# Second down phase built like the first: left factors from the stored hidden tiles, weight differences put aside earlier

## The chip, the cores and the metric

The kernel runs on one core of one Trainium2 chip. The metric is the time of one execution on the device in microseconds (us). Five engines with queues of their own take part: PE (TensorE, matmuls; PEld is its weight load), DVE (VectorE), ACT (ScalarE), POOL (GpSimd; here mainly the queue for stores) and SP (SyncE; the queue for loads). Transfers of all queues run on 16 DMA engines.

## The reference, cut to what matters

One residual block over 1024 tokens of width 1024; all float32:

```python
x = x + 0.5 * swiglu(rmsnorm(x, ffn1_norm), ffn1_w_gate, ffn1_w_up, ffn1_w_down)
x = x + hybrid_mixer(rmsnorm(x, mix_norm), ...)
x = x + 0.5 * swiglu(rmsnorm(x, ffn2_norm), ffn2_w_gate, ffn2_w_up, ffn2_w_down)
out = rmsnorm(x, final_norm)

def swiglu(h, w_gate, w_up, w_down):
    return (silu(h @ w_gate) * (h @ w_up)) @ w_down      # 1024 -> 2816 -> 1024
```

The change touches the last `swiglu` alone: how its hidden values (2816 x 1024 tokens) and `ffn2_w_down` (2816 x 1024) reach the last product.

## The kernel before, in words

**Precision.** A float32 operand is split into a rounded high part (a CAST on ACT, L169) and the rest (a subtraction on DVE, L170); a product is three matmuls (high by high, high by low, low by high), recorded at L91.

**Seven products.** Large matrix products are done in 2x2 blocks with seven products instead of eight (Strassen-Winograd). The factors are named P1, P2, P3, P5, P6, P7 and Q4. Three of the seven (P1, P2, P3) take blocks as they are on the right side, the other four take sums or differences. `Blocks.product` accumulates them in four PSUM banks, and small DVE and ACT steps combine the banks.

**Gate-up phase.** The 2816 hidden features are 22 tiles of 128. Three are made by plain products, two by a joint unit, and 17 one after another by a `Unit` of 84 matmuls of 128x512 (7 products x 4 k-tiles x 3). Gate and up weights come through `L` (`Loads`), two buffers named `raw`: a `raw` is loaded again when its last reader is done. `left` splits the weights and forms their sums (L482, L484, L485). Each unit leaves a hidden tile in two halves of 512 tokens. `Aside.take` gets them: two neighbouring tiles (a pair, 11 pairs in all) are combined by four subtractions or additions on DVE (L647), and the seven results are stored to the DRAM tensor `c_sp` from POOL (`put`, L644).

**Down phase.** `down` runs 16 turns. A turn is one group of 128 output rows and its partner four groups on, over two or three pairs: seven products in the order P1 P7 P5 P6 P2 Q4 P3, with 6 or 9 matmuls each (42 or 63 a turn, 924 in all). While a turn runs, `Prep` makes the left factors of the next turn and some right factors; the right factors of the first two pairs are made in the last unit of gate-up. Turns that are not the last of their group add their results to DRAM by accumulating stores from POOL (L835). Turns 12 to 15 are the last of their groups: they combine the banks with the loaded sums on DVE (L875) and hand the rows on (`ready`).

**The two down phases differ.** In the first (`i` = 0), the output rows are features: the left factors come from `ffn1_w_down`, four blocks loaded two turns ahead into `raw` and combined on DVE (L482, L484, L485); the right factors are the hidden differences read back from `c_sp[0]`, 512 columns at a time (`rights_back`, four tiles ahead). In the second (`i` = 1), the output rows are tokens. Its left factors are the hidden differences, read from `c_sp[1]` in pieces of 128 columns (`left_back`, L509: 7 x 2 or 3 pieces a turn, loaded within the turn ahead into the `w` tiles that the splits use). Its right factors come from `ffn2_w_down`, one 1 MB load for each pair into `raw`, with four DVE subtractions there (`rights_rows`, L771).

After each of the last turns, `to_output` squares, scales and stores rows of the final result (L1382 to L1402).

**What sets the order.** The program names its steps in the order of the functions below. The framework then fixes each engine's order when the program is built, by that order and by its own estimates of when operands and buffers will be there, so that an instruction may stand ahead of its place. On the chip each engine takes its instructions in that fixed order. `s` is a pool of 72 tiles of 128x512, `w` one of 10 tiles of 128x1024.

Of the kernel before, what the change touches and what calls it, by code (L numbers as in the profile page):

```python
# [41 lines left out]
def hybrid_block(ctx: ExitStack, tc: tile.TileContext, t: dict):  # L42
# [136 lines left out]
    class Loads:  # L179
# [14 lines left out]
        def take(self):  # L194
            return self.raw.pop(0)
# [176 lines left out]


# [10 lines left out]
    def ffn_weights(i, pre, nstd):  # L384
        wg, wu, wd = (t[f"{pre}_w_{n}"][0] for n in ("gate", "up", "down"))
        for m in range(int(i == 0), nstd):
            for w in (wg, wu):
                yield [part(0, w[:, m * P : (m + 1) * P])]
        for m in range(nstd, NF):
            yield [part(j * S, w[:, m * P : (m + 1) * P]) for j, w in enumerate((wg, wu))]  # L390
        for j, (g, q0, q1) in enumerate(TURNS):
            if i:
                continue
            n = (q1 - q0) * P
            rows = wd[2 * q0 * P : 2 * q1 * P].rearrange("(k two p) c -> two p k c", two=2, p=P)
            yield [(b * n, n, (lambda a: a.rearrange("p (k c) -> p k c", c=P)),
                    rows[two, :, :, d * P : (d + 1) * P])
                   for b, (two, d) in enumerate(((1, g), (0, g), (1, g + 4), (0, g + 4)))]
        for q in range(NQ * i):
            yield [part(0, wd[2 * q * P : 2 * (q + 1) * P])]  # L400

# [101 lines left out]
    def left_back(g, q0, q1):  # L503

        a = {}
        n = (q1 - q0) * P

        def load(to, i):
            nc.sync.dma_start(out=to.rearrange("p (k c) -> p k c", c=P),  # L509
                              in_=c_sp[1][i, q0:q1, :, g * P : (g + 1) * P].rearrange("k p c -> p k c"))  # L510

        def begin(i):
            raw = w4(F32)[:, : 2 * n]
            for j in range(2):
                load(raw[:, j * n : (j + 1) * n], i + j)
            return raw

        yield a
        raw = begin(0)
        yield  # L520
        for i, after_it in ((0, 4), (4, 2), (2, 6)):
            now = raw
            if after_it < 6:
                raw = begin(after_it)
            else:
                raw = s()[:, :n]
                load(raw, 6)
            parts = split(w4()[:, : 2 * n], w4()[:, : 2 * n], now)
            for j in range(2):
                a[FACTORS[i + j]] = tuple(x[:, j * n : (j + 1) * n] for x in parts)  # L530
            yield
        a["Q4"] = split(s(F32R)[:, :n], s(F32R)[:, :n], raw)
        yield

# [97 lines left out]

    class Aside:

        def __init__(self, i):
            self.sp, self.op = c_sp[i], ALU.add if i else ALU.subtract
            self.names = (("P1", "P5", "P2", "P3", "P7", "P6", "Q4"), ("P1", "P7", "P2", "Q4", "P5", "P6", "P3"))[i]
            self.raw = 0, 2, 3, (1 if i else None)  # L640
            self.even = {}

        def put(self, j, i, x):
            nc.gpsimd.dma_start(out=self.sp[FACTORS.index(self.names[i]), j], in_=x)  # L644
# [4 lines left out]

        def take(self, m, hf, x):  # L650
            j, odd = divmod(m, 2)
            if not odd:
# [3 lines left out]
                else:  # L656
                    self.e1 = x
                    self.t1 = self.comb(s(), self.e0, x, self.op)
# [4 lines left out]
            else:  # L663
# [3 lines left out]
                t3 = self.comb(self.e1, x, self.e1, self.op)  # L667
                self.put(j, 4, t3)
                t4 = self.comb(s(), t2, self.o0, self.op)
# [5 lines left out]
    def gate_up(i, act, started, nstd):  # L675
# [50 lines left out]
        for m in range(nstd + 2, NF):  # L726
# [4 lines left out]
            else:  # L731
                prep = iter(())
                makers[i] = Prep(i)
                makers[i].begin(0)
            for n, name in enumerate(FEW):
                unit.do(name)
                next(prep, None)
                if i in makers:
# [9 lines left out]
    def rights_back(ahead=4):  # L748
# [4 lines left out]
        def load():  # L753
            q, name = todo[len(raws)]
            raws.append(s())
            nc.sync.dma_start(out=raws[-1], in_=c_sp[0][FACTORS.index(name), q])
# [7 lines left out]
    def rights_rows():  # L764


        def done(name, x):
            b[name] = split(s(F32R), s(F32R), x)

        def comb(out, x, y, op):  # L770
            nc.vector.tensor_tensor(out=out, in0=x, in1=y, op=op)  # L771
            return out

        for q in range(NQ):
            b = ring[q] = {}
            raw, _ = L.take()
            b11, b12, b21, b22 = (raw[:, i * HALF : (i + 1) * HALF] for i in range(4))
            done("P1", b11)
            comb(b11, b11, b12, ALU.subtract)
            yield  # L780
            done("P7", comb(b12, b22, b12, ALU.subtract))
            yield
            done("P5", b11)
            yield
            done("P6", comb(b11, b11, b22, ALU.add))
            yield
            done("P2", b21)
            comb(b21, b11, b21, ALU.subtract)
            yield
            done("Q4", b21)  # L790
            yield
            done("P3", b22)
            L.load()
            yield

    class Prep:


        def __init__(self, i):
            self.i, self.made, self.lefts = i, 0, iter(())  # L800
            self.rights = rights_rows() if i else rights_back()
# [6 lines left out]
        def begin(self, j):  # L808
            if j < len(TURNS):
                g, q0, q1 = TURNS[j]  # L810
                self.lefts = left_back(g, q0, q1) if self.i else left(L.take()[0], (q1 - q0) * P, "P3")
# [619 lines left out]
```

## Time and profile before

| what | value |
|---|---|
| median of 3 runs | 1896.9 us (1896.22 to 1897.58) |
| the profiled execution's own time | 1896.36 us |
| its span, first to last instruction | 1894.7 us |
| mean granted TensorE clock | 0.986 |
| PE busy | 1833.0 us, 97% |
| DVE busy | 1381.2 us, 73% |
| ACT, POOL busy | 893.5 us, 252.4 us |

The engine rows overlap in time. What ends the execution is read from where the fullest engine, PE, does not run or runs slowly. The profiled execution lies 0.5 us under the median. The first down phase lies at about 474 to 689 us of the span, the second gate-up at about 1218 to 1641 us, the second down phase at 1641 to 1886 us.

### The profile page before, as it was taken

The numbers are of one execution on the slowest core, as the hardware profiler recorded it, in microseconds if no ns is written. First come the engines' busy times: TensorE is split into PE (matmuls) and PEld (weight loads), VectorE is DVE, ScalarE is ACT, GpSimd is POOL, SyncE is SP. The second block draws the span as 40 slices with busy tenths as digits, with TensorE's granted clock in tenths as the row PEclk, the third lists the DMA queues.
The fourth block names the chain that finished last, engine by engine and source line by source line (L and its number), as shares of the span: only waits on it lengthen the run. The fifth ranks groups of instructions, "written<-read, shape, count | busy, mean of one in ns | idle before, by whom it ended". The sixth has DMA issues, their size and how long they took to land.

```text
span 1894.7 us, 23205 instructions
## 1 busy us (share of the span) xinstructions
PE 1833.0 (97%) x8200; PEld 1508.1 (80%) x8200; DVE 1381.2 (73%) x2167; ACT 893.5 (47%) x1602; POOL 252.4 (13%) x400
## 2 busy tenths in 40 slices
PE   6999999999999999999999999999999999989997
PEld 5777888888888878888888878887888888777775
DVE  4788666666777797768787898658766666755768
ACT  3543222223555455667677775524322222344544
POOL 1201101010222221010101000210110101122211
PEclk8999999999999999999999999999999999999998
DMA  7213333334999853241313343412433333598985
GB/s 235 93 56 127 102 106 106 109 97 143 239 232 223 229 195 91 63 100 34 95 45 73 98 136 103 145 47 60 149 107 111 100 98 104 174 196 207 211 192 180
DMA packets 252933, 246.93 MB, mean 130 GB/s; under 512 B 14176, under 2 KB 197008, under 8 KB 252816
## 3 DMA queue, kind: packets, MB, share of 16 engines
q1 hardware_dynamic: 217072, 157.87, 27.8%
q0 software_dynamic: 35744, 87.58, 18.3%
q8 instruction: 64, 1.05, 0.2%
q14 instruction: 53, 0.43, 0.1%
HBM read 150.76 MB, written 85.20 MB: 125 GB/s over the span
## 4 chain that ended last, share of the span: by engine, by line
PE 68%; issue 15%; DVE 7%; DMA 4%; POOL 3%; ACT 1%; SPq 1%; POOLq 0%; DVEq 0%; ACTq 0%
PE ps L91 67%; DMA w<-c_sp 2%; DVE w L170 1%; DVE s L875 1%; POOL r_sp L835 1%; POOL c_sp L644 1%; DVE s L170 1%; DMA s<-c_sp 1%; DVE s L269 1%; PE ps L277 0%; DVE s L176 0%; POOL x_sp L835 0%; ACT w L169 0%; DMA r_sp<-s 0%; DMA raw<-in_ffn_w_gate 0%
## 5 line engine op out<-in xcount | busy, mean ns | idle before, releaser
L91 PE MATMUL ps<-s,w 128*128 128x512 f32 (+1 forms) x6400 | 1527.1, 393 | 38.6 <-ACT s L175 11.8
L91 PEld LDWEIGHTS ps<-s,w 128*128 128x128 f32 x6400 | 1198.2, 189 | 293.7 <-ACT s L175 12.7
L169 ACT CAST w<-raw 128x1024 fp32r<-128x1024 f32 (+2 forms) x158 | 157.5, 998 | 289.1 <-PE ps L91 189.1
L170 DVE TENSOR_TENSOR w<-raw,w 128x1024 fp32r<-128x1024 f32 (+2 forms) x158 | 182.0, 1153 | 109.4 <-PE ps L91 56.0
L91 PE MATMUL ps<-s,s 128*128 128x512 f32 (+3 forms) x944 | 241.4, 382 | 6.0 <-ACT s L858 4.3
L91 PEld LDWEIGHTS ps<-s,s 128*128 128x128 f32 x944 | 177.7, 189 | 46.1 <-ACT s L858 6.5
L644 POOL DMA_DIRECT2D c_sp<-s x154 | 83.5, 542 | 763.1 <-DVE s L630 579.8
L170 DVE TENSOR_TENSOR w<-w,w 128x768 fp32r<-128x768 f32 (+2 forms) x102 | 103.3, 1013 | 78.5 <-ACT w L169 39.3
L170 DVE TENSOR_TENSOR s<-s,s 128x512 fp32r<-128x512 f32 (+2 forms) x181 | 118.6, 670 | 39.8 <-ACT s L169 39.2
L169 ACT CAST w<-w 128x768 fp32r<-128x768 f32 (+2 forms) x102 | 89.6, 878 | 85.1 <-DMA w<-c_sp 39.3
L169 ACT CAST s<-s 128x512 fp32r<-128x512 f32 (+2 forms) x181 | 104.6, 607 | 43.4 <-DMA s<-c_sp 31.6
L626 ACT ACTIVATE s<-s 128x512 f32<-128x512 f32 x38 | 24.1, 633 | 190.0 <-DVE s L625 190.0
L170 DVE TENSOR_TENSOR s<-raw,s 128x512 fp32r<-128x512 f32 (+2 forms) x131 | 86.2, 666 | 25.9 <-ACT s L169 25.5
L482 DVE TENSOR_TENSOR w<-raw 128x1024 f32<-128x1024 f32 (+2 forms) x54 | 60.6, 1124 | 47.7 <-PE ps L91 46.7
L169 ACT CAST s<-raw 128x512 fp32r<-128x512 f32 (+2 forms) x131 | 76.7, 602 | 38.7 <-DVE raw L771 38.6
L611 ACT ACTIVATE s<-ps 128x512 f32<-128x512 f32 x38 | 22.7, 598 | 113.2 <-PE ps L91 113.2
L1254 DVE TENSOR_TENSOR s<-s,ps 128x128 f32<-128x128 f32 (+2 forms) x96 | 52.7, 548 | 16.8 <-ACT s L1250 16.4
L1242 ACT ACTIVATE s<-ps 128x128 f32<-128x128 f32 (+2 forms) x96 | 47.0, 490 | 37.7 <-PE ps L91 37.3
L835 POOL DMA_DIRECT2D r_sp<-s x48 | 41.6, 876 | 149.6 <-ACT s L854 48.3
L1250 ACT ACTIVATE s<-s 128x128 f32<-128x128 f32 (+2 forms) x96 | 50.2, 523 | 20.6 <-DVE s L1246 19.3
L617 DVE TENSOR_TENSOR s<-s,ps 128x512 f32<-128x512 f32 x38 | 26.0, 685 | 45.0 <-PE ps L91 45.0
L835 POOL DMA_DIRECT2D x_sp<-s x48 | 41.6, 866 | 126.3 <-DVE s L860 60.6
(133 smaller groups left out, 1697.6 us busy)
## 6 DMA issues: line engine op xcount, KB each, us to landing
c_sp<-s POOLq DMA_DIRECT2D x154, 256.0 KB, 2.5
raw<-in_ffn_w_gate SPq DMA_DIRECT2D x43, 512.0 KB, 3.9
raw<-in_ffn_w_up SPq DMA_DIRECT2D x43, 512.0 KB, 5.2
x_sp<-s POOLq DMA_DIRECT2D x80, 256.0 KB, 4.5
s<-c_sp SPq DMA_DIRECT2D x77, 256.0 KB, 7.1
r_sp<-s POOLq DMA_DIRECT2D x64, 256.0 KB, 5.1
w<-c_sp SPq DMA_DIRECT2D x72, 192.0 KB, 5.0
raw<-in_ffn_w_down SPq DMA_DIRECT2D x11, 1024.0 KB, 8.9
```

The costliest lines, as they stand in the source:

```text
L91: nc.tensor.matmul(out, lhs, rhs, **kw)
L169: nc.scalar.copy(hi, x)
L170: nc.vector.tensor_tensor(out=lo, in0=x, in1=f(hi), op=ALU.subtract)
L482: nc.vector.tensor_tensor(out=two(y), in0=two(blk(1, 2)), in1=blk(3).unsqueeze(1).to_broadcast([P, 2, n]), op=ALU.add)
L611: last_silu[0] = nc.scalar.activation(self.s0, o, AF.Silu)
L617: nc.vector.tensor_tensor(out=self.u3, in0=self.u2, in1=self.o[2], op=ALU.add)
L626: last_silu[0] = nc.scalar.activation(self.u2, self.u2, AF.Silu)
L644: nc.gpsimd.dma_start(out=self.sp[FACTORS.index(self.names[i]), j], in_=x)
L835: nc.gpsimd.dma_start(out=self.acc(self.g + 4 * i, hf), in_=x, accum_op=ALU.add)
L1242: behind(nc.scalar.activation(u["s"][:, cols], u["z"][:, cols], AF.Exp), table_set)
L1250: nc.scalar.activation(sc, sc, AF.Ln, bias=1.0)
L1254: nc.vector.tensor_tensor(out=sc, in0=sc, in1=u["z"][:, cols], op=ALU.max)
```

## The change

The second down phase takes the first one's code. `Aside.take` stores each half of a hidden tile as it is, to a new DRAM tensor `l_sp`, in four groups of 128 columns, and does no arithmetic for `i` = 1. `Loads` brings four blocks of `l_sp` for each turn into `raw`, and `left` combines them. The right factors that need a difference of `ffn2_w_down` are made in the gate-up phase: `weights` loads four 128x512 blocks after a unit's first product, `differences` makes four combinations on DVE after its sixth and stores them to `c_sp[1]`. This is done in 11 of the 17 single units. `rights_back` reads those back and takes P1, P2 and P3 from `ffn2_w_down` itself. `left_back` and `rights_rows` are gone.

```diff
+    l_sp = dr.tile([4, 4, P, NQ, P], F32, name="l_sp")
...
         for j, (g, q0, q1) in enumerate(TURNS):
+            n = (q1 - q0) * P
             if i:
+                yield [(b * n, n, (lambda a: a.rearrange("p (k c) -> p k c", c=P)), l_sp[b, g, :, q0:q1, :])
+                       for b in range(4)]
                 continue
...
-        for q in range(NQ * i):
-            yield [part(0, wd[2 * q * P : 2 * (q + 1) * P])]
...
-    def left_back(g, q0, q1):
...
-            nc.sync.dma_start(out=to.rearrange("p (k c) -> p k c", c=P),
-                              in_=c_sp[1][i, q0:q1, :, g * P : (g + 1) * P].rearrange("k p c -> p k c"))
...
+    wd2 = t["ffn2_w_down"][0]
...
+        def weights(self, j):
+            if not self.part or j >= NQ:
+                return
+            self.w = [s() for _ in range(4)]
+            for i in range(4):
+                nc.sync.dma_start(out=self.w[i], in_=wd2[(2 * j + i // 2) * P : (2 * j + i // 2 + 1) * P, hs(i % 2)])
+
+        def differences(self, j):
+            if not self.part or j >= NQ:
+                return
+            b11, b12, b21, b22 = self.w
+            t1 = self.comb(b11, b11, b12, ALU.subtract)
+            self.put(j, 1, t1)
+            t3 = self.comb(b12, b22, b12, ALU.subtract)
+            self.put(j, 4, t3)
+            t2 = self.comb(b22, t1, b22, ALU.add)
+            self.put(j, 5, t2)
+            t4 = self.comb(b21, t2, b21, ALU.subtract)
+            self.put(j, 6, t4)
+
         def take(self, m, hf, x):
             j, odd = divmod(m, 2)
+            if self.part:
+                nc.gpsimd.dma_start(out=l_sp[2 * hf + 1 - odd, :, :, j, :].rearrange("g p c -> p g c"),
+                                    in_=x.rearrange("p (g c) -> p g c", c=P))
+                return
...
+            pair = (m - nstd - 2) * NQ // (NF - nstd - 4)
+            odd = pair == (m - nstd - 1) * NQ // (NF - nstd - 4)
             for n, name in enumerate(FEW):
                 unit.do(name)
                 next(prep, None)
+                if n == 0 and not odd:
+                    out.weights(pair)
+                if n == 5 and not odd:
+                    out.differences(pair)
...
-            nc.sync.dma_start(out=raws[-1], in_=c_sp[0][FACTORS.index(name), q])
+            src = c_sp[part][FACTORS.index(name), q]
+            if part and name in ("P1", "P2", "P3"):
+                m = 2 * q + int(name != "P1")
+                src = wd2[m * P : (m + 1) * P, hs(int(name == "P3"))]
+            nc.sync.dma_start(out=raws[-1], in_=src)
...
-    def rights_rows():
...
-            self.rights = rights_rows() if i else rights_back()
+            self.rights = rights_back(i)
...
-                self.lefts = left_back(g, q0, q1) if self.i else left(L.take()[0], (q1 - q0) * P, "P3")
+                self.lefts = left(L.take()[0], (q1 - q0) * P, "P3")
```

Three places show how the fixed order moves. The first is PE at the start of the second down phase, in turn 1. Before, its P7 and P5 stand as follows (`ps` is the bank of a product, `w` a left factor, `s` a right factor; P7 goes to ps_14260, P5 to ps_14279):

```order
L91 MATMUL ps_14260<-s_13935,w_14172 128x512
L91 MATMUL ps_14260<-s_13936,w_14172 128x512
L91 MATMUL ps_14279<-s_13960,w_14172 128x512
L91 MATMUL ps_14279<-s_13961,w_14172 128x512
L91 MATMUL ps_14260<-s_13935,w_14173 128x512
L91 MATMUL ps_14260<-s_14050,w_14172 128x512
L91 MATMUL ps_14260<-s_14051,w_14172 128x512
L91 MATMUL ps_14260<-s_14050,w_14173 128x512
L91 MATMUL ps_14279<-s_13960,w_14173 128x512
L91 MATMUL ps_14279<-s_14054,w_14172 128x512
L91 MATMUL ps_14279<-s_14055,w_14172 128x512
L91 MATMUL ps_14279<-s_14054,w_14173 128x512
```

In the changed kernel the same two products of turn 1 (P7 in ps_14360, P5 in ps_14376):

```order
L91 MATMUL ps_14360<-s_14025,w_14262 128x512
L91 MATMUL ps_14360<-s_14026,w_14262 128x512
L91 MATMUL ps_14360<-s_14025,w_14263 128x512
L91 MATMUL ps_14360<-s_14145,w_14262 128x512
L91 MATMUL ps_14360<-s_14146,w_14262 128x512
L91 MATMUL ps_14360<-s_14145,w_14263 128x512
L91 MATMUL ps_14360<-s_14249,w_14262 128x512
L91 MATMUL ps_14360<-s_14250,w_14262 128x512
L91 MATMUL ps_14360<-s_14249,w_14263 128x512
L91 MATMUL ps_14376<-s_14049,w_14262 128x512
L91 MATMUL ps_14376<-s_14050,w_14262 128x512
L91 MATMUL ps_14376<-s_14049,w_14263 128x512
```

Before, the two products are cut into pieces and put in turns, with their third pair's matmuls (not in these rows) pushed behind turn 0's remaining products; now each runs whole, nine matmuls in a row, as in the first down phase. From turn 1 to turn 12, nearly all runs of the changed kernel are nines.

The second place is SP's queue of loads in the middle of that down phase (turns 9 to 11). Before:

```order
L509 DMA w_15335<-c_sp_80 128x3x128 x2
L509 DMA w_15350<-c_sp_80 128x3x128 x2
L509 DMA w_15369<-c_sp_80 128x3x128 x2
L509 DMA s_15387<-c_sp_80 128x3x128
L191 DMA raw_15322<-in_ffn_w_down 128x2x1024
L509 DMA w_15449<-c_sp_80 128x3x128 x2
L509 DMA w_15464<-c_sp_80 128x3x128 x2
L509 DMA w_15483<-c_sp_80 128x3x128 x2
L509 DMA s_15506<-c_sp_80 128x3x128
```

and in the changed kernel:

```order
L191 DMA raw_15408<-l_sp 128x384 x4
L760 DMA s_15431<-c_sp_80 128x512
L760 DMA s_15449<-c_sp_80 128x512
L191 DMA raw_15533<-l_sp 128x384 x4
L760 DMA s_15562<-c_sp_80 128x512
L760 DMA s_15615<-in_ffn_w_down 128x512
L760 DMA s_15657<-c_sp_80 128x512
```

The loads into `w` tiles are gone. Left blocks now go into `raw`, four to a turn, and right factors into `s` tiles, one at a time.

The third place is DVE in a single gate-up unit. Before, around the hidden tiles' L647 (L614 to L630 combine a unit's banks):

```order
L630 SCALAR_TENSOR_TENSOR s_12268<-s_12268,s_12213 128x512
L647 TENSOR_TENSOR s_12326<-s_12307,s_12268 128x512
L614 TENSOR_TENSOR s_12342<-s_12342,ps_12348 128x512
L170 TENSOR_TENSOR w_12381<-raw_12157,w_12380 128x1024
L617 TENSOR_TENSOR s_12397<-s_12342,ps_12384 128x512
```

and in the changed kernel, in a unit that handles a pair of weight rows (L583 is the old L614, L586 the old L617; L617 is now the weights' combination):

```order
L583 TENSOR_TENSOR s_12333<-s_12333,ps_12347 128x512
L617 TENSOR_TENSOR s_12339<-s_12339,s_12340 128x512
L617 TENSOR_TENSOR s_12340<-s_12342,s_12340 128x512
L170 TENSOR_TENSOR w_12380<-raw_12150,w_12379 128x1024
L617 TENSOR_TENSOR s_12342<-s_12339,s_12342 128x512
L617 TENSOR_TENSOR s_12341<-s_12342,s_12341 128x512
L586 TENSOR_TENSOR s_12396<-s_12333,ps_12383 128x512
```

The four weight combinations stand early in the unit, between the second and the fourth product's steps, and not at the sixth, where the code has them.

## Rows read from the trace of the kernel before

**Rows 1.** The page's head, and busy time with share of span.

```profile
span 1894.7 us, 23205 instructions
PE 1833.0 (97%) x8200; PEld 1508.1 (80%) x8200; DVE 1381.2 (73%) x2167; ACT 893.5 (47%) x1602; POOL 252.4 (13%) x400
```

**Rows 2.** Busy time by stretch: both down phases, to turn 12's Q4, then on.

```profile
core 0: us, PE busy (x) PEld busy (x) DVE busy (x) ACT busy (x) POOL busy (x), PEclk, DMA share, GB/s
473.60:654.30 180.70, 180.36 (x793) 148.37 (x792) 131.79 (x200) 98.93 (x170) 44.28 (x53) 1.00 0.94 232
1640.60:1844.40 203.80, 188.11 (x793) 150.67 (x792) 134.31 (x199) 100.27 (x172) 44.34 (x53) 0.97 0.86 205
654.30:689.30 35.00, 34.01 (x149) 27.51 (x147) 34.73 (x61) 12.87 (x22) 7.09 (x13) 1.00 0.64 210
1844.40:1886.40 42.00, 37.06 (x145) 28.68 (x143) 39.82 (x83) 19.09 (x46) 5.40 (x6) 0.92 0.64 196
```

**Rows 3.** Timeline of PE: one row of the first down, three of the second.

```profile
570.14 12.40 PE L91 MATMUL ps<-s,w 128*128 128x512 f32 x54
...
1683.99 2.82 PE L91 MATMUL ps<-s,w 128*128 128x512 f32 x11 [2.79 <-ACT w L169]
...
1812.10 3.84 PE L91 MATMUL ps<-s,w 128*128 128x512 f32 x9 [4.03 <-DVE s L845]
...
1884.85 1.53 PE L91 MATMUL ps<-s,w 128*128 128x512 f32 x6
```

**Rows 4.** Waits from 1600 us on: engine, line, releaser; us, times, longest.

```profile
ACT w L169 <- DMA w<-c_sp: 39.3, 13, 9.4
ACT s L169 <- DVE raw L771: 38.6, 26, 4.1
DVE w L170 <- ACT w L169: 31.6, 13, 10.2
PE ps L91 <- DVE s L845: 9.2, 4, 4.0
```

**Rows 5.** Chain of waits, two of its longest pieces in the second down.

```profile
1796.70 12.10 DMA w<-c_sp
...
1812.10 18.16 PE ps L91 x72
```

**Rows 6.** DVE groups by shape: second down (first row), first down (the others).

```profile
L771 DVE TENSOR_TENSOR raw<-raw 128x512 f32<-128x512 f32 x40 | 27.6, 689 | 0.8
...
L482 DVE TENSOR_TENSOR w<-raw 128x512 f32<-128x512 f32 x3 | 2.0, 681 | 0.0
...
L484 DVE TENSOR_TENSOR raw<-w,raw 128x256 f32<-128x256 f32 x3 | 1.3, 417 | 0.0
```

**Rows 7.** DMA issues: count, KB of one, median us to landing.

```profile
c_sp<-s POOLq DMA_DIRECT2D x154, 256.0 KB, 2.5
...
s<-c_sp SPq DMA_DIRECT2D x77, 256.0 KB, 7.1
r_sp<-s POOLq DMA_DIRECT2D x64, 256.0 KB, 5.1
...
raw<-in_ffn_w_down SPq DMA_DIRECT2D x11, 1024.0 KB, 8.9
raw<-in_w_in SPq DMA_DIRECT2D x16, 256.0 KB, 3.2
```

**Rows 8.** The loads of L509: landing, shortest, median and longest.

```profile
DMA to landing us min/median/max: 2.3/4.5/12.8
```

**Rows 9.** Six single units of the second gate-up; below, L647 alone there.

```profile
1373.38:1487.62 114.24, 114.24 (x505) 94.59 (x504) 75.25 (x97) 31.66 (x42) 11.38 (x21) 1.00 0.33 105
...
1373.38:1487.62 114.24, 7.76 (x12) 1.00 0.33 105
```

**Rows 10.** Timeline at a unit's start: a DVE row, and POOL's put of the finished tile.

```profile
1457.97 0.69 DVE L614 TENSOR_TENSOR s<-s,ps 128x512 f32<-128x512 f32 x1
...
1456.29 0.54 POOL L644 DMA_DIRECT2D c_sp<-s  x1 [4.29 <-DVE s L630]
```

More of the change, by code (lines that the diff above doesn't have):

```diff
@@ L391, in ffn_weights @@
         for j, (g, q0, q1) in enumerate(TURNS):
+            n = (q1 - q0) * P
             if i:
+                yield [(b * n, n, (lambda a: a.rearrange("p (k c) -> p k c", c=P)), l_sp[b, g, :, q0:q1, :])
+                       for b in range(4)]
                 continue
-            n = (q1 - q0) * P
             rows = wd[2 * q0 * P : 2 * q1 * P].rearrange("(k two p) c -> two p k c", two=2, p=P)
@@ L500, in left @@
         L.load()
-        yield
-    def left_back(g, q0, q1):
-        a = {}
-        n = (q1 - q0) * P
-        def load(to, i):
-            nc.sync.dma_start(out=to.rearrange("p (k c) -> p k c", c=P),
-                              in_=c_sp[1][i, q0:q1, :, g * P : (g + 1) * P].rearrange("k p c -> p k c"))
[L512 to L532, printed above, removed]
         yield
@@ L631, in store @@
             self.out(hf, u)
+    wd2 = t["ffn2_w_down"][0]
     class Aside:
         def __init__(self, i):
[L638 to L641, printed above, removed]
+            self.part = i
+            self.names = ("P1", "P5", "P2", "P3", "P7", "P6", "Q4")
         def put(self, j, i, x):
-            nc.gpsimd.dma_start(out=self.sp[FACTORS.index(self.names[i]), j], in_=x)
+            nc.gpsimd.dma_start(out=c_sp[self.part][FACTORS.index(self.names[i]), j], in_=x)
         def comb(self, out, x, y, op):
@@ L657, in take @@
                     self.e1 = x
-                    self.t1 = self.comb(s(), self.e0, x, self.op)
+                    self.t1 = self.comb(s(), self.e0, x, ALU.subtract)
                     self.put(j, 1, self.t1)
@@ L666, in take @@
                 self.put(j, 5, t2)
-                t3 = self.comb(self.e1, x, self.e1, self.op)
+                t3 = self.comb(self.e1, x, self.e1, ALU.subtract)
                 self.put(j, 4, t3)
-                t4 = self.comb(s(), t2, self.o0, self.op)
+                t4 = self.comb(s(), t2, self.o0, ALU.subtract)
                 self.put(j, 6, t4)
@@ L746, in hybrid_block, with rights_back @@
     ORDER = ("P1", "P7", "P5", "P6", "P2", "Q4", "P3")
-    def rights_back(ahead=4):
+    def rights_back(part, ahead=4):
         todo = [(q, name) for q in range(NQ) for name in ORDER]
@@ L762, in rights_back @@
             yield
-    def rights_rows():
[L767 to L794, printed above, removed]
     class Prep:
```

## The prediction

> **What bounds the kernel now.** I read first the busy times: PE runs in 97% of a span of 1894.7 us [rows 1], so time is won only where PE stands still or runs at a lower clock. Next I compared the two down phases stretch by stretch, because they issue the same 924 matmuls and the change gives the second the code of the first. I cut each behind Q4 of turn 12, where the last turns begin to hand out rows. The reader should see in [rows 2] that the same 793 matmuls took a stretch of 180.70 us in the first phase and 203.80 us in the second. Of those 23.1 us, 15.4 are idle time (203.80 - 188.11 = 15.7 against 180.70 - 180.36 = 0.3) and 7.75 are slower matmuls (188.11 against 180.36), at a granted clock of 0.97 against 1.00. Where that comes from the timeline shows [rows 3]: 54 matmuls in 12.40 us in the first phase are 0.230 us each; after a gap of 4.03 us in the second, nine take 3.84 us, 0.427 each. So a gap is paid nearly twice, once as idle time and once in the clock behind it.
>
> What the gaps wait for is in the waits [rows 4]. PE names DVE's L845 (the sum on a product's bank), 9.2 us in four waits, but L845 is only queued there: DVE waited 31.6 us for ACT's casts of left factors, and ACT 39.3 us for the loads of L509, the longest 9.4 us. The chain has the same load as a piece of 12.10 us, and right behind it PE's long run [rows 5]. The loads of L509 land after 2.3 to 12.8 us [rows 8] and are issued within the turn ahead. It is their lateness, not a shortage of transfer rate: the first phase kept the DMA engines busier (0.94 against 0.86) and moved more (232 against 205 GB/s) without gaps [rows 2].
>
> The tails after the cut take 35.00 and 42.00 us. In both DVE is nearly full (34.73 of 35.00, 39.82 of 42.00) [rows 2], so there DVE's work is the bound, and the second phase has more of it (83 instructions against 61), because the final output is made in it.
>
> **The change part by part.**
>
> *The body of the second down phase.* left_back's loads go, and with them the 39.3 us that ACT waited [rows 4]. In their place stand, as in the first phase, four block loads a turn, two turns ahead, three combinations on DVE, and one right factor at a time, four tiles ahead. PE's order becomes the first phase's, in clean runs of nine. The bytes are those of before: the 16 turns run over 44 pairs in all, of 64 KB a block, so the left factors go from 7 x 44 x 64 KB to 4 x 44 x 64 KB, 8.25 MB less (in units of 1024), and the right ones from 11 x 1 MB to 77 x 256 KB, 8.25 MB more. DVE loses the four subtractions of L771 for each pair, 0.689 us each, and gains three combinations a turn (0.681 + 2 x 0.417 = 1.5 us) [rows 6]; the first phase's DVE total is 131.79 us in 180.70 with exactly those [rows 2]. The nearest row for the new body is thus the first phase's, whole: 180.70. I take all of it: **-23.1 us**. What differs from the first phase: the left blocks come in runs of 1 to 1.5 KB, and three of seven right loads come from the weights themselves. Bounds: if only the idle time goes and the clock stays at 0.97, -15.4; if all goes, -23.1.
>
> *The tail.* DVE is the bound, so each of its instructions counts. Added are the combinations of the left factors of the last two turns, 2 x 1.5 = 3.0 us. Gone are two splits of right factors that the old order still had there, about 0.65 us each (an operation of that size took 0.69 [rows 10]), 1.3 us together. So **+1.7 us**, between 0 (all covered by the 2.2 us in which DVE idled) and +3.0.
>
> *The gate-up units, DVE.* Six units take 114.24 us, 19.04 each, with PE busy all the time and DVE for 75.25, 12.54 a unit [rows 9]. The subtractions of hidden tiles (L647, 7.76 us in six units, 0.647 each) go: -1.29 a unit. In 11 of 17 units four come back at that price: +2.59. A unit with weights then has 13.84 us of DVE work, 5.2 under PE's 19.04; the cover is there, and the sum gets **0**. Without cover it would be 11 x 1.3 = 14 us.
>
> *The gate-up units, a new wait.* The weights' first combinations stand right behind the unit's second bank step, early, and the loads that they need go into `s` tiles that come free only when the unit ahead has put its last hidden half away. Behind the waiting DVE instruction are queued the unit's splits and bank steps, for which PE waits. POOL starts the put of that half at 1456.29 [rows 10]. From there: the put lands 2.5 (to `c_sp`) to 5.1 us (to `r_sp`) later, being issued costs SP at most 0.9 more, as long as a store takes POOL, and a load of 256 KB lands 3.2 us (weights, in this phase) to 7.1 us (in a down phase) after that [rows 7]. That is 1462.9 to 1469.4. DVE would be ready for it at about 1457.97 + 0.69 + 0.65 = 1459.3 [rows 10]. So a stall of 3.6 to 10.1 us in a unit; I take about 4, since the DMA engines are busy for 0.33 of the time here [rows 9] and the short landings belong to this phase. 13.84 + 4 = 17.8 us is still under 19.04: **0**. At the upper end it is 23.9, or 4.9 too much; the unit after it, if it has no weights, has 19.04 - 11.25 = 7.8 us to catch up, but two of three have them, so about 2 x 4.9 + 4.9 - 7.8 = 6.9 us are lost in four units, some 24 us in all. That would eat the gain.
>
> *The gate-up units, stores.* Seven puts a pair become four, and four more for the weights; a put keeps POOL for 0.54 us [rows 10], and POOL is busy for 11.38 of 114.24 [rows 9]. The hidden puts now go out in runs of 512 bytes, four times as many. Nobody waits for them until the down phase; if each cost POOL four times as much, it would still be under half busy. **0**.
>
> *A rule against it.* In the rows, the first phase made 77 loads of 256 KB, 7.1 us median to landing [rows 7], beside 0.3 us of idle PE [rows 2]; with four in flight that is 77 x 7.1 / 4 = 137 us, under 180.7. The old 1 MB loads landed after 8.9 us [rows 7]. The Trainium skill, page "DMA: Bandwidth & Descriptors", section "Rules for kernel authors", asks for 1 MiB or more per DMA for the highest bandwidth, and its section "Anatomy of one DMA — SWDGE (gpsimd) path" fits one DMA as 2 us plus its bytes over 436 GB/s; by that, as an estimate, eleven loads of 1 MB would need 48 us of queue time, and 77 of 256 KB 200 us, if one after another. By the rule the right factors would become late; by the rows they do not. I go by the rows, and keep the other as rival D.
>
> **Sum.** 1896.4 (the profiled execution's own time, 1.7 over its span) - 23.1 + 1.7 + 0 = 1875.0; the median of the runs is 0.5 higher than that execution, so 1875.5, and I say 1875.
>
> **Rivals.** 0.2%, 3.8 us, is about what a measurement of this kernel can tell from no change.
>
> A. The forecast, 1870 to 1880: the body between 180 and 185 us, the tail 42 to 45. Chance 0.72.
>
> B. Gate-up takes part back, in stalls of 6 to 8 us in the weights' units, or the body loses only the idle time (1875.5 + 7.7 = 1883). 1881 to 1891. For it: put and load in a row, never shown in the profile before. Against: the 5.2 us of room. 0.10.
>
> E. More is won: the tail's DVE work spreads and the tail comes near the first phase's 35 us, -7: 1868. For it: the old tail had 2.2 us of idle DVE, and a clock of 0.92. Against: 22 more DVE instructions. 0.08.
>
> D. The change does not do what it says: the loads of right factors become the late ones. If the body's 63 such loads landed after 12.8 us, the longest of [rows 8], four at a time, they would need 63 x 12.8 / 4 = 202 us, the old body. About 1896, within 0.2%. Against: the first phase. 0.05.
>
> C. Slower: the wait in the units decides. The point is a weight load that lands over 7.1 us after a put of 5.1 (stall over 10 us): there the 24 us of gate-up equal the gain. At 12.8 us to landing the stall is 15.8, a unit overshoots by 10.6, and four units lose 3 x 10.6 - 7.8 = 24 us, over 80 in all: 1930 or more. Against: the landings of 3.2 us in this phase. 0.05.
>
> The 8 in 10 range takes A, E and most of B: 1867 to 1886. Faster 0.90 (A, B, E), same 0.05 (D), slower 0.05 (C).
>
> **What the profile after would show.** Right: the body of the second down near 180.7 us with a granted clock of 1.00; no waits for loads into `w`; runs of nine matmuls without gaps; the tail 42 to 45 us with DVE nearly full; a unit's period still 19.04 us, and DVE's waits for weight loads under 5 us each. Wrong: a period over 19.04 in units with weights (B, C); ACT waiting for `s` or `raw` loads in the second down (D); a tail near 35 (E). The weakest step is the one on the put and load in a row, since nothing in the profile before shows that wait.

## The result and the profile after

The changed kernel takes 1870.95 us (median of four runs, 1868.80 to 1873.41) against 1896.99: a ratio of 0.9865, 95% interval 0.9853 to 0.9876, or 26.0 us less. The forecast was 1875, in a range of 1867 to 1886.

The head of the page after, to set beside [rows 1]:

```profile
span 1869.1 us, 23411 instructions
PE 1819.1 (97%) x8200; PEld 1502.6 (80%) x8200; DVE 1379.8 (74%) x2171; ACT 892.7 (48%) x1602; POOL 267.1 (14%) x411
```

PE's share is 97% as before; it is the span that is 25.6 us shorter. Where they went is seen in stretches. Windows of the kernel after: the first 60 us of the second down's body, the rest of it up to turn 12's Q4, and from there to the end (columns as in [rows 2]).

```profile
1638.97:1698.97 60.00, 60.00 (x266) 49.70 (x265) 44.91 (x69) 34.86 (x60) 14.89 (x18) 1.00 0.94 235
1698.97:1818.49 119.52, 119.52 (x529) 98.95 (x528) 84.50 (x128) 62.57 (x108) 27.89 (x33) 1.00 0.94 229
1818.49:1869.10 50.61, 34.67 (x145) 26.30 (x143) 44.27 (x93) 21.27 (x49) 7.18 (x8) 0.92 0.45 149
```

The same three windows of the kernel before:

```profile
1640.60:1700.60 60.00, 53.94 (x226) 42.84 (x225) 39.17 (x59) 30.71 (x52) 13.71 (x18) 0.97 0.87 215
1700.60:1844.36 143.76, 134.13 (x568) 107.79 (x567) 95.09 (x142) 69.52 (x120) 30.63 (x36) 0.98 0.86 201
1844.36:1894.70 50.34, 37.10 (x145) 28.72 (x143) 43.39 (x90) 22.01 (x51) 7.18 (x8) 0.89 0.59 185
```

The body went from 203.8 to 179.5 us, with PE never idle and a granted clock of 1.00. A matmul costs 119.52 / 529 = 0.226 us there; by that price the kernel before lost (266 - 226) x 0.226 = 9.0 us in its first 60 us and the other 15.2 of 24.2 in the rest. The last stretch, this time up to the end of the span, stayed as it was: 50.34 and 50.61. The remaining 1.6 us lie ahead of the down phase, and are mostly chance (below). Sum: -1.6 - 24.2 + 0.3 = -25.5, against 25.6 in the spans.

The waits after, from 1600 us on (columns as in [rows 4]):

```profile
DVE s L170 <- ACT s L169: 25.5, 16, 2.7
ACT s L169 <- DMA s<-in_ffn_w_down: 16.3, 10, 3.6
DVE w L170 <- ACT w L169: 11.3, 6, 2.0
PE ps L91 <- DVE s L817: 2.7, 3, 1.6
```

ACT's waits for loads into `w` (39.3 us before) are gone. ACT now waits 16.3 us for right factors loaded from `ffn2_w_down`, at most 3.6 at a time (and 6.7 us for those from `c_sp`), and PE does not notice: its waits for the bank sums (L817, the old L845) fell from 9.2 to 2.7 us, all in the last stretch.

A gate-up unit still takes 19.04 us. Six of them, four with weights, to set beside [rows 9]:

```profile
1372.41:1486.65 114.24, 114.24 (x505) 94.60 (x504) 77.82 (x101) 31.67 (x42) 17.80 (x28) 1.00 0.49 157
```

### The profile page after: what moved, and what is told of

Same layout as the page of the kernel before. It is cut to its first block, busy times and chain, and to the rows that moved or that the text cites. A ratio compares the mean times of both kernels' runs of the same rounds, so it can differ in the third digit from the quotient of the medians.

```text
span 1869.1 us, 23411 instructions
## 1 busy us (share of the span) xinstructions
PE 1819.1 (97%) x8200; PEld 1502.6 (80%) x8200; DVE 1379.8 (74%) x2171; ACT 892.7 (48%) x1602; POOL 267.1 (14%) x411
## 4 chain that ended last, share of the span: by engine, by line
PE 84%; DVE 7%; DMA 4%; issue 2%; ACT 1%; SPq 1%; POOL 0%; POOLq 0%; DVEq 0%; ACTq 0%
PE ps L91 82%; DMA s<-c_sp 2%; DVE s L847 2%; DVE w L170 1%; DVE s L170 1%; DMA raw<-in_ffn_w_gate 1%; DVE s L269 1%; DVE s L176 1%; DVE s L513 1%; SPq L191 0%; PE ps L277 0%; ACT w L169 0%; PE ps L1072 0%; DMA s<-in_x 0%; SPq L896 0%
## 5 line engine op out<-in xcount | busy, mean ns | idle before, releaser
L91 PEld LDWEIGHTS ps<-s,w 128*128 128x128 f32 x6400 | 1193.9, 189 | 275.2 <-ACT s L175 12.8
L169 ACT CAST w<-raw 128x1024 fp32r<-128x1024 f32 (+2 forms) x190 | 182.5, 961 | 311.2 <-PE ps L91 227.5
L170 DVE TENSOR_TENSOR w<-raw,w 128x1024 fp32r<-128x1024 f32 (+2 forms) x190 | 210.2, 1107 | 104.8 <-ACT w L169 63.6
L170 DVE TENSOR_TENSOR s<-s,s 128x512 fp32r<-128x512 f32 x242 | 162.8, 684 | 52.4 <-ACT s L169 51.5
L169 ACT CAST s<-s 128x512 fp32r<-128x512 f32 x242 | 143.2, 618 | 54.5 <-DMA s<-c_sp 26.4
L614 POOL DMA_DIRECT2D c_sp<-s x121 | 65.7, 543 | 419.4 <-DVE s L599 288.6
L483 DVE TENSOR_TENSOR w<-raw 128x1024 f32<-128x1024 f32 (+2 forms) x70 | 74.8, 1069 | 57.9 <-PE ps L91 53.6
L595 ACT ACTIVATE s<-s 128x512 f32<-128x512 f32 x38 | 24.0, 633 | 189.3 <-DVE s L594 189.3
L170 DVE TENSOR_TENSOR w<-w,w 128x1024 fp32r<-128x1024 f32 (+2 forms) x70 | 74.9, 1070 | 52.9 <-PE ps L91 42.1
L169 ACT CAST w<-w 128x1024 fp32r<-128x1024 f32 (+2 forms) x70 | 64.8, 925 | 46.5 <-DVE w L483 40.7
L643 POOL DMA_DIRECT2D l_sp<-s x44 | 33.2, 755 | 322.4 <-DVE s L599 260.9
L583 DVE TENSOR_TENSOR s<-s,ps 128x512 f32<-128x512 f32 x38 | 26.1, 686 | 47.9 <-issue 25.6
L617 DVE TENSOR_TENSOR s<-s,s 128x512 f32<-128x512 f32 x88 | 58.7, 687 | 1.3
```

What stands on the lines that cost most here:

```text
L91: nc.tensor.matmul(out, lhs, rhs, **kw)
L169: nc.scalar.copy(hi, x)
L170: nc.vector.tensor_tensor(out=lo, in0=x, in1=f(hi), op=ALU.subtract)
L483: nc.vector.tensor_tensor(out=two(y), in0=two(blk(1, 2)), in1=blk(3).unsqueeze(1).to_broadcast([P, 2, n]), op=ALU.add)
L614: nc.gpsimd.dma_start(out=c_sp[self.part][FACTORS.index(self.names[i]), j], in_=x)
L643: nc.gpsimd.dma_start(out=l_sp[2 * hf + 1 - odd, :, :, j, :].rearrange("g p c -> p g c"), in_=x.rearrange("p (g c) -> p g c", c=P))
```

## Experiments

Eleven variants ran, and the changed kernel a second time. "Body", "start" (us lost in its first 60), "rest" and "last" (from turn 12's Q4 to the end) come from windows as above. Start is 266 less the matmuls of the first 60 us, times 0.226; rest is what else the body has over 179.5. Where matmul records are missing and the clock was 1.00 behind the first 60 us, rest is the idle time there instead (marked i), and start is what is left. Each variant was profiled in one execution, which is one of its runs; those of e9 and e10 lie 3.9 and 4.8 us above the medians of their kernels, so that their bodies may be some us shorter in other runs. The median of the kernel before moved by 3 us from one set of runs to another, so each kernel is read by its ratio to the runs of before beside it. Every edit also lets the framework fix the engines' orders anew; that was not held apart, except as e10 bears on PE's.

| kernel | median us | ratio to before (95%) | body | start | rest | last |
|---|---|---|---|---|---|---|
| before | 1897.0 | 1 | 203.8 | 9.0 | 15.2 | 50.3 |
| after | 1871.0 | 0.9865 (0.9853 to 0.9876) | 179.5 | 0 | 0 | 50.6 |
| e8 before, small right loads | 1888.9 | 0.9964 (0.9951 to 0.9977) | 192.9 | 10.1 | 3.3 i | 50.3 |
| e1 lefts only | 1884.2 | 0.9929 (0.9912 to 0.9945) | 189.3 | 8.1 | 1.7 i | 50.8 |
| e9 three pairs aside | 1872.5 | 0.9878 (0.9856 to 0.9899) | 180.0 | 0.2 | 0.3 | 52.4 |
| e2 rights only | 1882.0 | 0.9922 (0.9908 to 0.9937) | 189.9 | 5.0 | 5.4 | 49.8 |
| e3 old lefts in raw | 1877.8 | 0.9907 (0.9886 to 0.9928) | 185.1 | 5.4 | 0.1 | 49.7 |
| e10 before, three pairs aside | 1890.9 | 0.9978 (0.9960 to 0.9996) | 200.8 | 4.3 | 17.0 | 50.4 |
| e4 two tiles ahead | 1901.8 | 1.0023 (1.0012 to 1.0034) | 206.1 | 10.4 | 16.2 | 53.1 |
| e5 more DVE in units | 1873.1 | 0.9881 (0.9849 to 0.9912) | 180.0 | 0.5 | 0 | 52.4 |
| e7 gain on POOL | 1874.8 | 0.9890 (0.9875 to 0.9904) | 179.8 | 0 | 0.3 | 53.1 |
| e6 one scale | 1869.4 | 0.9869 (0.9850 to 0.9887) | 179.6 | 0 | 0.1 | 49.4 |
| e11 three pairs, one scale | 1869.0 | 0.9856 (0.9825 to 0.9888) | 179.5 | 0 | 0 | 48.3 |
| after, again | 1872.5 | 0.9878 (0.9846 to 0.9909) | 179.9 | 0 | 0.4 | 49.8 |

**e1: new left factors, differences made in the down phase.**

```diff
-                if n == 0 and not odd:
-                    out.weights(pair)
-                if n == 5 and not odd:
-                    out.differences(pair)
...
-            self.rights = rights_back(i)
+            self.rights = rights_rows() if i else rights_back(i)
```

`rights_rows` here is that of before, on four 256 KB loads a pair into `s` tiles.

> Left factors as in the changed kernel (raw blocks of l_sp, two turns ahead), but the differences of the down weights are made in the down phase again, by DVE from four 256 KB loads a pair; nothing of them in the gate-up units. Theory (the gain is that left factors are no longer loaded late): second down body up to turn 12's Q4 at 180 to 185 us against 203.8 before and 179.5 after, total 1868 to 1877. Rival (the gain comes from the right factors and PE's clean order, which this kernel does not have: its fixed PE order is cut in the first turns and now and then later): body 195 to 204, total 1885 to 1897.

Neither: 189.3 and 1884.2, between the two. Windows of e1's body, the first 60 us and the rest:

```profile
1643.46:1703.46 60.00, 53.02 (x218) 41.07 (x217) 46.04 (x70) 31.66 (x54) 12.71 (x15) 0.97 0.74 177
1703.46:1832.71 129.25, 127.58 (x561) 104.97 (x561) 108.00 (x166) 68.79 (x119) 30.18 (x35) 1.00 0.80 184
```

After its first 60 us the body has 1.7 us of idle PE; at the start it loses 8.1, nearly as much as before. The chain at that start (start, length, what):

```profile
1648.97 0.87 DVE w L483
1649.84 0.60 DVE s L170
...
1650.96 0.68 DVE s L779
...
1666.58 0.56 DVE s L170
1667.16 0.33 SPq L191
...
1667.54 6.14 DMA raw<-l_sp
```

It goes through DVE piece after piece (L779 is the subtraction of weights; DVE was busy for 23.2 of the phase's first 25 us, against 21.9 in the kernel after), and then through a left load that could be issued only behind DVE's split, at 1667.16. Late left factors are not the whole cause.

**e2: new right factors, old left ones.** `left_back`, the hidden sums and their stores (to `h_sp`) as before; `rights_back` as in the change.

> Right factors as in the changed kernel (differences put aside in the gate-up units, 77 loads, PE's order in clean nines), but the left factors as before: hidden sums made in gate-up, 112 loads within the turn ahead into w tiles. Theory (late left loads are the cause): ACT again waits for loads into w, 25 us or more, body 198 to 206, total 1888 to 1898. Rival (rights and order are the cause): waits into w stay but PE does not feel them, body 180 to 186, total 1870 to 1877.

Between again: 189.9. ACT waits 28.0 us for loads into `w`, as the theory had it, but at most 4.1 at once (9.4 before), and the body loses 10.4 us, not 24. So each half of the change alone gives over half of the body's gain (14.5 and 13.9 of 24.2): the causes overlap.

**e3: the old left pieces, loaded into `raw`.**

```diff
-        raw = begin(0)
+        (x, _), (y, _) = L.take(), L.take()
+        for i, raw in ((0, x[:, : 2 * n]), (4, x[:, 2 * n : 4 * n]), (2, y[:, : 2 * n])):
```

> The same as the kernel with only the rights changed, but the seven left pieces of a turn are loaded into the two raw buffers, about half a turn to a turn before they are split, not into w tiles. Still 112 loads from stored hidden sums in 512-byte runs. Theory (lateness, set by the buffer they wait for): no waits for them, body 180 to 185, total 1870 to 1877. Rival (112 loads in short runs are too slow for the queues in themselves): body stays above 195, total 1885 or more.

185.1 and 1877.8, just outside the theory's ranges, and its "no waits for them" did not come true:

```profile
ACT w L169 <- DMA raw<-h_sp: 20.7, 6, 6.5
```

But past the first 60 us PE does not feel them: it has 125.07 us of work in 125.07. So with a buffer early, 112 loads in 512-byte runs cost PE nothing there. What stays is a start of 5.4 us. The chain to its longest gap (3.4 us, up to 1668.44) runs over two right loads from `c_sp` (4.07 and 5.35 us) and then a left load that was issued late, at 1660.95, and took 5.11 us.

**e4: two right tiles ahead.**

```diff
-            while len(raws) < min(len(todo), i + ahead):
+            while len(raws) < min(len(todo), i + (2 if part else ahead)):
```

> The changed kernel with right factors of the second down loaded two tiles ahead and not four. Theory of the prediction (77 loads by their landing of 7.1 us, two in flight: 77 x 7.1 / 2 = 273 us of loads against a body of 180): ACT waits for right loads, body 195 to 270, total 1886 or more. Rival (landing is long only because four are in flight and DMA is full; with two each lands in 3 to 4 us, 77 x 3.5 / 2 = 135): body 180 to 185, total 1869 to 1877.

The first holds, and the rival falls: ACT waits 37.9 us for right loads from the weights alone. Loads of the second down, two tiles ahead (columns as in [rows 7]):

```profile
s<-c_sp SPq DMA_DIRECT2D x38, 256.0 KB, 6.6
...
s<-in_ffn_w_down SPq DMA_DIRECT2D x29, 256.0 KB, 6.4
```

With four ahead the same loads landed after 7.6 and 7.9 us. Half as many in flight made a load only some 15% quicker, so the row of loads takes 67 x 6.5 / 2 = 218 us, near the body's 206. The fixed order of PE is cut in this kernel too, and what either costs was not held apart.

**e8: the kernel before with its 1 MB loads cut.** What stood ahead of the late left loads shows in SP's issues of the kernel before (L191 is the 1 MB load of weight rows, L509 the left loads; start, length, what):

```profile
1795.73 0.37 SPq L191 DMA_DIRECT2D raw<-in_ffn_w_down  x1
1796.15 15.49 SPq L509 DMA_DIRECT2D w<-c_sp  x6
```

The load that took 12.10 us [rows 5] starts at 1796.70, 1.0 us behind a 1 MB load in the same queue. e8 cuts each 1 MB load into four, one at each of four steps:

```diff
-            raw, _ = L.take()
-            b11, b12, b21, b22 = (raw[:, i * HALF : (i + 1) * HALF] for i in range(4))
+            b11, b12, b21, b22 = raws[q]
...
             done("P7", comb(b12, b22, b12, ALU.subtract))
+            load(q + 1)
             yield
```

> The kernel before, but each pair's 1 MB load of down-weight rows is four loads of 256 KB, one at each of four steps of the pair ahead, into s tiles; left factors and the four subtractions as before. In the trace of before the late left loads stand in SP's queue right behind such a 1 MB load (1795.73 and then 12.10 us to landing). Theory A (the 1 MB load ahead of them makes them late): ACT's waits for loads into w fall from 39 us to under 20, none over 5; the body past its first 60 us loses under 5 us against 15 before; total 1884 to 1889. Theory B (the w tiles come free late, whatever is loaded ahead): waits and total as before, 1893 to 1900.

Theory A, nearly throughout; the wait's sum was mis-sized. The wait in e8, the landing of the left loads (to set beside [rows 8]), and the body's first 60 us and its rest:

```profile
ACT w L169 <- DMA w<-c_sp: 25.3, 9, 4.9
...
DMA to landing us min/median/max: 2.1/4.4/7.4
...
1643.96:1703.96 60.00, 53.49 (x219) 41.13 (x218) 38.77 (x58) 30.29 (x52) 14.01 (x18) 0.97 0.84 199
1703.96:1836.89 132.93, 129.59 (x565) 105.09 (x563) 95.86 (x142) 69.53 (x120) 30.22 (x35) 1.00 0.93 221
```

The sum fell from 37.9 us (in the same window of the kernel before, 1630 to 1850 us) only to 25.3, but the longest wait from 9.4 to 4.9 and the longest landing from 12.8 to 7.4, while the median landing stayed (4.5 and 4.4). With the long ones gone, the rest of the body loses 3.3 us, not 15.2. The left loads are as many and as large as before, and the bytes are the same. Whether a left load waits for the 1 MB load in SP's queue or at the DMA engines that all queues share is not shown. (The total gained less, 6.7 us: the body begins 3.4 us later, with 1.9 us of idle PE ahead of the last unit's Q4.)

**e9 and e10: the differences of three pairs put aside.** e9 is the changed kernel with the other eight made in the down phase as in e1; e10 is the kernel before with its 1 MB loads for the other eight.

```diff
-            if not self.part or j >= NQ:
+            if not self.part or j >= 3:
```

> The changed kernel with the weight differences put aside in gate-up for the first three pairs alone; the other eight are made in the down phase by DVE from four 256 KB loads a pair. The kernel with only the left factors changed lost its time in the first 60 us of the body, where DVE works without a pause (46 of 60 us) on the rights of the first pairs. Theory (differences made early matter only for the start): the first 60 us of the body without idle PE, total 1869 to 1875. Rival (they matter all along): the body past its start loses 5 us or more, total 1877 to 1885.

> The kernel before (left factors from stored hidden sums into w tiles, 1 MB loads of weight rows), but the differences of the first three pairs are put aside in gate-up; the other eight come from 1 MB loads in the down phase. Theory (two separate causes: DVE's work for the first pairs at the start, about 9 us; the 1 MB loads ahead of the left loads afterwards, about 10 us, and the left loads themselves, about 5): the loss of the first 60 us falls from 9 to at most 5 us, that of the rest stays 12 us or more; total 1888 to 1894. Rival (one cause, the left loads, shows at the start too): start and total as before, 1894 to 1900.

Both theories hold. e9 has the whole gain, within the interval of its ratio, with 3 of 11 pairs aside. Its body, the first 60 us and the rest:

```profile
1642.38:1702.38 60.00, 59.97 (x265) 49.33 (x264) 48.21 (x74) 33.01 (x57) 13.59 (x16) 1.00 0.81 202
1702.38:1822.35 119.97, 119.97 (x531) 99.22 (x530) 99.15 (x152) 64.84 (x112) 29.27 (x34) 1.00 0.81 188
```

e10 halves the loss of the start and keeps that of the rest (17.0), although its order of PE, as built, is in clean nines from turn 2 on: the order by itself gives little.

**e5: twelve more additions on DVE in each unit with weights.**

```diff
+            x = s()
+            for _ in range(12):
+                self.comb(x, t2, t4, ALU.add)
```

> The changed kernel with twelve more DVE additions of 128x512 (0.65 us each, result unused) in each of the 11 units with weights: 13.84 + 7.8 = 21.6 us of DVE work against the unit's 19.04. Theory of the prediction (DVE's work in the units is free while it is under 19.04, and above that what is over is lost, less what a unit without weights makes up, 7.8 us): about 2 x 2.6 over in two of three units, 7.8 to spare in the third, so 0 to 10 us lost, total 1871 to 1881. Rival 1 (PE waits in each unit for all that is over): 11 x 2.6 = 28 us, total about 1899. Rival 2 (there was no cover, every added DVE instruction counts): 11 x 7.8 = 86 us, total about 1957.

1873.1 beside 1872.5 of the changed kernel on the same chip. Six units of e5:

```profile
1371.28:1485.52 114.24, 114.24 (x505) 94.59 (x504) 104.97 (x152) 31.78 (x42) 18.95 (x30) 1.00 0.50 162
```

DVE has 104.97 of 114.24 us, and PE is never idle: what the units of 21.6 us have over 19.04 is made good by the units without weights.

**e7: the final gain on POOL.**

```diff
-        nc.vector.tensor_tensor(out=r, in0=r, in1=gb[hf], op=ALU.mult)
+        nc.gpsimd.tensor_tensor(out=r, in0=r, in1=gb[hf], op=ALU.mult)
```

> The changed kernel with the 16 multiplications by the final gain (0.68 us each on DVE, 10.9 in all) made by POOL. Theory (DVE bounds everything from turn 12's Q4 to the end, 50.6 us): that stretch shortens by 6 to 10.9 us, total 1860 to 1865. Rival (PE or the chain of loads, squares and scales is the bound there, or POOL is as late): 0 to 3 us, total 1868 to 1875.

The theory missed, and the total lies in the rival's range: the stretch became 53.1 us, though 16 instructions of DVE with 10.9 us of work were gone. DVE in e7's last stretch (columns as in [rows 6]):

```profile
L847 DVE TENSOR_TENSOR s<-s,ps 128x512 f32<-128x512 f32 x18 | 11.9, 678 | 0.0
L1371 DVE TENSOR_SCALAR s<-s,sm 128x512 f32<-128x512 f32 x8 | 6.9, 867 | 3.7 <-POOL sm L1367 3.4
L170 DVE TENSOR_TENSOR w<-raw,w 128x512 fp32r<-128x512 f32 x4 | 5.3, 1328 | 0.0
```

and the same lines in the kernel after:

```profile
L847 DVE TENSOR_TENSOR s<-s,ps 128x512 f32<-128x512 f32 x18 | 12.1, 679 | 0.0
L1371 DVE TENSOR_SCALAR s<-s,sm 128x512 f32<-128x512 f32 x8 | 3.9, 484 | 2.2 <-POOL sm L1367 2.2
L170 DVE TENSOR_TENSOR w<-raw,w 128x512 fp32r<-128x512 f32 x5 | 3.4, 684 | 0.0
```

The subtractions of L170 with both inputs in SBUF went from 684 to 1328 ns and the scales of L1371 from 484 to 867, those with one input in PSUM stayed at 679. Within a line it is the instructions beside a POOL multiplication that are longer: an L170 at 1838.81 took 1.78 us beside one, an L170 at 1832.60, with none, 0.69. The Trainium skill, page "SBUF — State Buffer", section "Who interferes with whom", says that a DVE instruction with two SBUF inputs contends with a GpSimd instruction that reads SBUF and one with at most one such input, outside the two-port modes, does not; the rows agree. The longer instructions took back what the move gave: DVE's work in the stretch is 44.87 us, against 44.27 in the kernel after.

**e6 and e11: gain and scale in one DVE instruction**, in e11 with three pairs aside.

```diff
+            nc.vector.scalar_tensor_tensor(out=r, in0=r, scalar=inv, in1=gb[hf], op0=ALU.mult, op1=ALU.mult)
```

> The changed kernel with the final gain and the row scale in one DVE instruction for each half row block (16 of about 0.69 us after the power, in place of 16 of 0.68 before it and 8 of 0.48 after; ACT's 8 scales go too). DVE has about 3.9 us less in the last stretch. Theory (DVE bounds it): 2 to 4 us less, total 1866 to 1869. Rival (the last power and scales now stand one behind the other at the end): no gain or 1 us more, total 1871 to 1873.

> Weight differences put aside for three pairs alone, and gain and row scale in one DVE instruction. By the runs of either part: body as in the changed kernel (179 to 181 us), last stretch about 49.5 us, total 1867 to 1871. Rival (the DVE work that came back into the down phase delays the last stretch, which was 52.35 us with three pairs aside): 1871 to 1875.

> The changed kernel once more, on the same chip as the runs beside it: 1869 to 1873. Every stretch as in its first profile: body 179 to 181 us, from turn 12's Q4 to the end 50 to 51.5.

The changed kernel, run again, came out as expected but for its last stretch (49.8, 0.2 short of the range). e6's last stretch is 49.4 us, between its theory and its rival: 1.2 less in one profile, while two profiles of the changed kernel differ by 0.8; its ratio, 0.9869, shows no gain on the changed kernel's 0.9865. e11's last stretch is 48.3, and its four runs (1866.7 to 1869.4) lie below the four of the changed kernel beside them (1871.3 to 1873.9), by 3.5 us of medians. The intervals of the two ratios overlap, so e11 is probably a little faster, not surely. Of the 4.6 us between the two profiled spans 2.7 lie ahead of the down phase, 0.4 in the body and 1.5 in the last stretch.

## Why the prediction was right, and where its reasons were not

The forecast was 21.4 us less and the spans differ by 25.6: 1.1 more than forecast in the body, 1.4 in the tail, and 1.6 ahead of the down phase, for which the forecast had nothing.

**The body, -23.1.** It measured -24.2. Taking the first phase's stretch whole gave the right size, for reasons that were in part wrong. The prediction's "a gap is paid nearly twice" is too much by its own totals, 7.75 us of slower matmuls on 15.4 of idle time; that matmuls are slow behind a gap holds (in the 1.9 us behind the gap of 4.03 us the granted clock was 0.50, the lower of its two levels). The step "left_back's loads go, and with them the 39.3 us that ACT waited" put all of it down to the left loads and their being issued within the turn ahead. The runs split it, one edit at a time: before to e8 (1 MB loads cut) 10.8 us of body, e8 to e1 (new left factors; the small loads come four at a time) 3.7, e1 to e9 (three pairs' differences early) 9.3, e9 to after 0.5; together 24.2 before rounding. In another order the shares would be others, since the causes overlap. The latest of the left loads were late because of the 1 MB loads ahead of them, and the left loads alone do not explain the nine us at the start: new left factors without early differences leave 8.1 of them (e1). No run has the new left factors beside the 1 MB loads, so whether issuing the left loads two turns ahead would by itself have borne those is open. The rows hinted at both: [rows 7] has the 1 MB loads at 8.9 us to landing, and [rows 4] ACT's 38.6 us of waits for L771, to which the prediction gave no price. That sum is no measure of the loss, though: e1 has 34.8 us of such waits in the same part of the kernel, and loses 9.7.

What at the start is DVE's work and what the cut order is not settled: in e1 and e9 both differ. A full DVE can't be all of it: in the kernel before DVE was busy for only 19.7 of the phase's first 25 us, and the start lost 9.0. With the order in nines and old left factors (e2, e3, e10) 4.3 to 5.4 us stay; in e3 the chain there runs over loads (above), but no run takes these apart.

**The tail, +1.7.** Cut at the last matmul, as the prediction cut it, it fell from 42.0 to 40.0, outside the 42 to 45 that it gave as a sign; up to the end of the span, where DVE still works, it is +0.3. The added combinations are there and the two splits of right factors are gone, but one split of a left factor moved ahead of the cut as well: in the last stretch DVE has 44.27 us of work, 0.9 more than before. The cut was the flaw: where DVE works on for 6.6 us behind PE's last matmul, that matmul is no mark. Profiles of kernels with the same tail code (the changed kernel twice, e5 and e9) gave 49.8 to 52.4, so +0.3 and +1.7 can't be told apart, nor is it shown that each DVE instruction counts there. Rival E is not what happened.

**The units, DVE, 0.** Right: DVE's work in six units, four with weights, should be 6 x 11.25 + 16 x 0.647 = 77.85; it measured 77.82. And e5 shows the cover to be larger than the 5.2 us a unit that were claimed.

**The units, the put and load in a row, a stall of about 4.** No such stall is seen: DVE's waits that end with these loads are four, 4.3 us in all, and PE stood still for none of them. The loads are issued at a unit's start (L191's lines ahead are gate and up weights):

```profile
1387.95 0.58 SPq L191 DMA_DIRECT2D raw<-in_ffn_w_up  x1
1388.62 2.30 SPq L625 DMA_DIRECT2D s<-in_ffn_w_down  x4
```

and used by DVE 12 us later, after 4.8 to 6.5 us to landing:

```profile
1400.47 1.41 DVE L617 TENSOR_TENSOR s<-s,s 128x512 f32<-128x512 f32 x2
```

The put of the last hidden half started at 1398.19: the loads did not wait for it. The step that `s` tiles come free only with that put was wrong, and harmless. Two of its numbers were wrong as well. The 3.2 us "in this phase" are of loads from `in_w_in`, which run at 671 to 1014 us, in the mixer; here the median is 5.2, by which the stall would have been 5.6 us and a unit 0.4 us too long. And with two units in three overfull, as it says, the loss at the upper end is 2 x 4.9 - 7.8 = 2.0 us in three units, not 6.9 in four; rival C's sum has the same slip. Rival C and the first condition of B hung on that step and fall with it.

**The stores, 0.** A put in four groups keeps POOL for 0.76 us, not 0.54, and lands after 2.8, not 2.5. Free.

**Rival D, the rule of large transfers.** With four in flight it fell. With two, in e4, the loads of right factors are late and the kernel is no faster than before (1.0023), as the rival had it.

## What to carry to other kernels

A large load can be a delay for the small loads issued behind it, as here: read the issues of the queue just ahead of a late landing before blaming the late load. When one phase runs clean and its twin does not, the clean one's time is a good forecast of the other, but the reasons still have to be found edit by edit, since waits that end on one engine overlap. Here the work for the phase's first steps was worth moving ahead; for the later steps it was free where it stood.

## What was not expected of the hardware

The same 82 matmuls of the first single unit of the second gate-up, behind the same gap of 1.33 us, took 18.94 us in one execution of the changed kernel and 20.46 in another. From the timeline of the first:

```profile
1289.35 18.94 PE L91 MATMUL ps<-s,w 128*128 128x512 f32 x82 [1.33 <-DVE s L170]
```

and of the second:

```profile
1289.03 20.46 PE L91 MATMUL ps<-s,w 128*128 128x512 f32 x82 [1.33 <-DVE s L170]
```

The granted clock over these matmuls was 1.00 in the first and 0.92 in the second; why is not known. Of the fourteen profiled executions, three have the short one (18.94 to 18.99: the changed kernel's first, e6 and e11), and the kernel before has 20.49. The second execution of the changed kernel comes to the down phase at 1639.94, 1.0 us later than the first, so that most of the 1.6 us gained ahead of the down phase is chance and not the change. And a load of 256 KB in the busy down phase took 6.5 us with two right loads in flight and 7.7 with four: halving their number took off only 1.2 us. What else makes such a load slow was not tried.
